# Late position steps of a Fourier mixing layer: spectra requested between the two residual blocks, and VectorE's rows in another order

## The chip, the core and the metric

The kernel runs on one core of a Trainium2 chip. Its engines are TensorE (PE: matmuls, with PEld for its weight loads), VectorE (DVE), ScalarE (ACT), GpSimd (POOL) and SyncE (SP); each works through its own list of instructions in order, and an instruction that has to wait holds up everything behind it on that engine. SP, and here and there ACT and POOL, also issue DMAs. The metric is the device time of one execution in microseconds (us).

## The reference

Two sequences (2048 and 512 positions, 1024 channels, float32) go through two layers and a last norm:

```python
def trunk(x, ...):
    x = x + (banded_gqa_with_sink(q, k, v, ...) * silu(gate)) @ w_out   # layer 0, h = rmsnorm(x)
    f = fftn(h in 4 groups of 256 channels, axes=(position, channel), norm="ortho").real
    x = x + (f * silu(h @ w_gate)) @ w_out                               # layer 1, h = rmsnorm(x)
    return rmsnorm(x, final_norm)
```

The change touches only the end of layer 1: the transform over positions, the gate, the out-projection, the residual sum and the last norm.

## The kernel before

**Arithmetic.** A float32 product is made of three matmuls on rounded halves. An operand's high half is a cast on ACT, its low half the remainder, a subtraction on DVE (`halves_of` L1394 to L1408: ACT L1403, DVE L1404; `split` L1015; `own` L1523 and L1524). `matmul3` (L117) multiplies high by high, high by low and low by high, so the second of every three matmuls on TensorE needs the low half.

**The transform over 2048 positions** is split by 16. Earlier steps leave, for each k1 of 0 to 8, two blocks of 128 x 1024 (real and imaginary part of the spectra: `g1r`, `g1s` and so on, made on DVE by the sums and differences of `pm`, L1261). A position step for k1 turns these into the two row blocks k1 and 16-k1. The order of k1 is 0 and 8, 4, 2, 6, 1, 7, 3, 5; the last four, k1 = 1, 7, 3, 5, are the loop at L1844 and are called the late position steps here. The spectra of k1 = 7, 3 and 5 wait their turn in DRAM (`god`): ACT issues their six writes (L1824) during step 6, and `reads` (L1835 to L1842) brings one pair back per step as four DMAs of 256 KB on SP (L1841, tiles `go`).

One late step does this:
1. `halves_of` gives the operands `gp_<half>_<0 or 1>`: half 0 and 1 are channels 0 to 511 and 512 to 1023, 0 and 1 the real and the imaginary spectrum.
2. `position` (L1412 on): for each half, six matmuls of 260 columns and six of 256 with the table `tbp` into PSUM (`ABp_0`, `ABp_1`); copies, sums and differences on ACT and DVE give two blocks `up` (L1441 to L1448); DVE multiplies each by its gate (L1451, `s2p`).
3. PE transposes both in half blocks (`tw`, L95). From them come the operands of the out-projection: `tT` (own halves), `F` (sums), `S` (split sums).
4. The out-projection of the two blocks is done together in `Outs.products` (L1565 on), in the manner of Strassen and Winograd, as seven products of four times three 512-column matmuls; their PSUM tiles are `Wo`, `Zo` and `Xo`. DVE adds each to the residual blocks `xa` and `xb` (L1572; the trace calls them `x`, the order `x_1`, `x_15` by their row blocks).
5. Last norm: ACT squares and sums (`jkf`, L1056), DVE scales the sum (`invf`, L110), POOL raises it to the power -1/2 (L111), DVE scales the block (L1468), SP writes it out (L1470).

The steps are woven together: while step k's seven products run on PE, step k+1's operands are made and its `ABp` matmuls stand between the products. The last product of a step goes into `xb`'s lower half; this sum, the late sum, and xb's norm fall into the following step.

**What sets the order.** A scheduler puts the program into one list per engine; `after` and `seq` (L159 to L168) add dependencies of order alone, with chains "dve" and "act" through the late steps. SP's DMAs go out in the order of its list: one that waits for a buffer or for a block to be ready holds up those behind it. Buffers come from small pools: four tiles `x` are shared by residual blocks and gate tiles, the spectra and `up` blocks share the pool of `zt`, and PSUM has three accumulators (`psum2`) for `Wo`, `Zo`, `Xo` and the earlier `fo`.

`fo` are the plain out-projections of step 2's two blocks (`finish`, L1484 on), 24 matmuls of 512 columns for each half block; step 6's `ABp` matmuls are placed among them.

Of the kernel before, what the change touches and what calls it, by code (L numbers as in the profile page):

```python
# [42 lines left out]
def encoder(  # L43
# [947 lines left out]
    def fourier_phase(tail):  # L991
        with ExitStack() as es:
# [481 lines left out]
            def normed(x2, r):  # L1474
                norm(x2, r)()

            def residual(r):
                x2 = x_tile(f"x2_{r[0]}")
                SP.dma_start(x2, rows(x1d, r))
                return x2  # L1480

            late = [None]
# [1 line left out]
            def finish(uT, r, between=None):  # L1484
                r0 = r[0]
                x2 = residual(r)
                for half in range(2):
                    if half and between:
                        chain["turns"] = end
                        between()  # L1490
                    ps = psum2.tile([P, 512], F32, tag="acc", name=f"fo{r0}_{half}")
                    for k in range(KD):
                        first_one = k == 0 and half == (between is not None)
                        end = matmul3(
                            ps, uT[k], wo[half * KD + k], k == 0, k == KD - 1, behind=chain.get("turns") if first_one else None
                        )
                    xs = x2[:, half * 512 : half * 512 + 512]
                    DVE.tensor_tensor(xs, xs, ps, ALU.add)
                if between:
                    late[0] = x2, r  # L1500
                else:
                    normed(x2, r)
                return end
# [3 lines left out]
            class Outs:  # L1507
# [57 lines left out]
                def products(self, hooks, last=False):  # L1565
# [48 lines left out]
                        upper()  # L1614
                    if not last:
                        prod(W, A[1, 1], ft["N4"], four, False)
                        seq("dve", add(xb, 0, W))
                        return xb, self.us[1][1]
                    ss = main.tile([P, 8], F32, tag="ss", bufs=2, name="ssl")
                    junk = fp.tile([P, 512], F32, tag="c12", bufs=1, name="jkl").bitcast(BF16)  # L1620

# [193 lines left out]
            o0s, o1s = pm(tsn[1], tsn[3], "o0s")  # L1815
            g1r, g7r = pm(e0c, o0c, "g1r")
            g1s, g7s = pm(o0s, e0s, "g1s")
            g3r, g5r = pm(e1c, o1s, "g3r")
            p6 = [halves_of("p6", *G[6], 0), None]
            g5s, g3s = pm(o1c, e1s, "g5s")  # L1820
            G[1], G[7], G[3], G[5] = (g1r, g1s), (g7r, g7s), (g3r, g3s), (g5r, g5s)
            for k1 in (7, 3, 5):
# [22 lines left out]
            for k1, k2 in ((1, 7), (7, 3), (3, 5), (5, None)):  # L1845
# [3 lines left out]
                def split_g():  # L1849

                    nxt["s"] = [gated(name, r, place) for r, place in zip(tiles, (xtile, left))]
                    scaled = []

                    def weigh():
                        if late[0]:
                            scaled.append(norm(*late[0], "dve"))

                    nxt["p"] = [halves_of(name, *gl, 0, weigh), None]
                    o.rest()
                    for f in scaled:  # L1860
                        f()
                    if not ft["T3"]:
                        f_sums("T3", right)

                def transform(third):
                    if not ft["N4"]:
                        f_sums("N4", left)
                    nxt["p"][1] = halves_of(name, *gl, 1)
                    nxt["o"] = Outs(k1, position(name, k1, *gl, tiles, (nxt["s"], tb), nxt["p"], third))

                def turns():
                    nxt["o"].operands()
                    nxt["o"].load()
                    if k2:
                        nxt["r"] = reads(k2)

                late[0] = o.products((split_g, transform, turns, lambda: nxt["o"].others()))
                o = nxt["o"]
            o.products((lambda: (o.rest(), normed(*late[0])), lambda third: third(), lambda: None), last=True)


    fourier_phase(attention_phase())
# [98 lines left out]
```

## Time and profile before

| | |
|---|---|
| runs | 1584.42, 1585.3 and 1582.39 us, median 1584.42 |
| the profiled execution | 1583.8 us, of which span 1582.0 us |
| TensorE clock granted | 0.999 |
| PE, DVE, ACT, POOL busy | 99%, 73%, 56%, 28% of the span |
| `ABp` matmuls of step 6 | 1428.12 to 1441.6 us |
| of steps 1, 7, 3, 5, the first at | 1460.72, 1485.39, 1511.46, 1536.27 us |

Times in the trace count from the span's start. A line of a timeline reads: start, length, engine, source line, operation, output<-input, shape, how many in the group, and in brackets how long the engine had stood idle ahead of it and on what. Lengths overlap a little where an engine is pipelined, so distances between starts tell more than single lengths.

### The profile page before, as it was taken

How to read it: one execution, taken by the hardware profiler on the slowest of the kernel's cores; microseconds unless marked ns; L12 is line 12 of the kernel's file. 1: busy time of each engine (PE TensorE's matmuls, PEld its weight loads, DVE VectorE, ACT ScalarE, POOL GpSimd, SP SyncE). 2: the span in 40 equal slices, each digit the busy share in tenths (PEclk: the TensorE clock that was granted, in tenths of full speed). 3: DMA queues.
4: the chain of work that ended last, by engine and by line, in shares of the span. 5: the costliest groups of instructions: out<-in, count | busy, mean ns of one | idle time of the engine just before them, and what ended most of it. 6: DMA issues, size and time to landing. Idle time of an engine off the chain costs nothing.

```text
span 1582.0 us, 27728 instructions
## 1 busy us (share of the span) xinstructions
PE 1568.8 (99%) x9882; PEld 1315.8 (83%) x9882; DVE 1151.3 (73%) x2793; ACT 878.1 (56%) x2096; POOL 444.2 (28%) x614
## 2 busy tenths in 40 slices
PE   9999999999999999999999999999999999999998
PEld 7888888888888888988888888888888888887776
DVE  6888556877457886378764577669778878988886
ACT  7788535776246784267751576546555554343343
POOL 2475642421404314024222242223112121111110
PEclk9999999999999999999999999999999999999999
DMA  8597686575856567665659566675557569448752
GB/s 302 205 331 280 227 356 210 210 266 194 303 202 225 207 234 271 214 221 210 251 172 326 205 231 231 236 259 196 191 213 253 180 228 411 171 181 313 278 180 81
DMA packets 100997, 373.91 MB, mean 236 GB/s; under 512 B 11267, under 2 KB 22283, under 8 KB 83452
## 3 DMA queue, kind: packets, MB, share of 16 engines
q1 hardware_dynamic: 83148, 298.17, 52.9%
q0 software_dynamic: 16400, 70.04, 11.4%
q10 hardware_dynamic: 1312, 3.94, 0.7%
q8 instruction: 78, 1.28, 0.3%
q14 instruction: 59, 0.48, 0.1%
HBM read 280.84 MB, written 91.26 MB: 235 GB/s over the span
## 4 chain that ended last, share of the span: by engine, by line
PE 91%; DVE 4%; DMA 2%; ACT 1%; issue 1%; POOL 0%; POOLq 0%; SPq 0%; DVEq 0%; ACTq 0%
PE gp L117 14%; PE qp L117 14%; PE spt L117 11%; PE op L117 7%; PE W L117 7%; PE av L615 6%; PE spt L530 6%; PE fo L117 4%; PE vp L117 3%; PE Z L117 3%; PE pt L589 3%; PE Wo L117 2%; PE z L117 2%; PE X L117 2%; PE ABp L117 1%; PE Zo L117 1%
## 5 line engine op out<-in xcount | busy, mean ns | idle before, releaser
L117 PE MATMUL gp<-h,wg 128*128 128x512 f32 x960 | 237.7, 396 | 0.0
L117 PE MATMUL qp<-h,wq 128*128 128x512 f32 x960 | 237.1, 396 | 0.0
L549 DVE CUSTOM_DVE_ANT_0 S<-spt,b 128x385 f32<-128x385 f32 (+1 forms) x320 | 156.6, 528 | 105.7 <-PE spt L530 68.4
L117 PEld LDWEIGHTS gp<-h,wg 128*128 128x128 f32 x960 | 174.9, 188 | 37.2 <-issue 1.0
L117 PEld LDWEIGHTS qp<-h,wq 128*128 128x128 f32 x960 | 174.9, 188 | 36.6 <-issue 0.2
L557 ACT ACTIVATE S<-S 128x385 f32<-128x385 f32 (+1 forms) x320 | 188.8, 597 | 19.6 <-DVE S L549 19.3
L597 ACT CAST pts<-pt 128x384 fp32r<-128x384 f32 (+1 forms) x240 | 100.5, 457 | 167.6 <-PE pt L589 158.4
L598 DVE TENSOR_TENSOR pts<-pt,pts 128x384 fp32r<-128x384 f32 (+1 forms) x240 | 114.3, 520 | 23.7 <-ACT pts L597 22.7
L117 PE MATMUL spt<-wo,uT 128*128 128x512 f32 x480 | 120.3, 391 | 0.0
L639 POOL TENSOR_TENSOR uT<-o,uT 128x256 fp32r<-128x256 f32 x75 | 55.5, 740 | 229.8 <-ACT uT L638 229.7
L117 PE MATMUL op<-wo,uT 128*128 128x512 f32 x480 | 118.9, 391 | 0.0
L530 PE MATMUL spt<-kwin,qab 64*128 64x384 f32 (+1 forms) x960 | 118.5, 353 | 0.0
L615 PEld LDWEIGHTS av<-pts,v 128*128 128x128 f32 x576 | 101.4, 188 | 18.8
L615 PE MATMUL av<-pts,v 128*128 128x512 f32 (+1 forms) x576 | 115.7, 341 | 0.0
L117 PE MATMUL fo<-wo,tTu 128*128 128x512 f32 x480 | 115.5, 392 | 0.0
L117 PEld LDWEIGHTS op<-wo,uT 128*128 128x128 f32 x480 | 89.4, 188 | 18.5
L117 PEld LDWEIGHTS spt<-wo,uT 128*128 128x128 f32 x480 | 89.1, 188 | 18.3
L117 PEld LDWEIGHTS fo<-wo,tTu 128*128 128x128 f32 x480 | 88.3, 188 | 17.5 <-ACT wo L1722 0.3
L569 DVE TENSOR_SCALAR S<-S 128x384 f32<-128x384 f32 (+1 forms) x192 | 95.8, 499 | 6.8
L530 PEld LDWEIGHTS spt<-kwin,qab 64*128 64x128 f32 x960 | 74.5, 186 | 28.2 <-issue 26.4
L635 POOL TENSOR_TENSOR o<-o,s 128x256 f32<-128x256 f32 x75 | 55.3, 737 | 134.4 <-DVE o L633 134.0
L589 PEld LDWEIGHTS pt<-ident,S 64*128 64x128 f32 x1328 | 78.2, 138 | 4.3 <-issue 2.0
(331 smaller groups left out, 3178.5 us busy)
## 6 DMA issues: line engine op xcount, KB each, us to landing
wo<-wsd SPq DMA_DIRECT2D x32, 1024.0 KB, 4.9
wq<-wsd SPq DMA_DIRECT2D x31, 1024.0 KB, 6.6
wg<-wsd SPq DMA_DIRECT2D x31, 1024.0 KB, 5.3
x<-x1d SPq DMA_DIRECT2D x40, 512.0 KB, 3.5
b<-b21d SPq DMA_DIRECT2D x40, 512.0 KB, 6.6
b<-rowd SPq DMA_DIRECT2D x40, 384.0 KB, 4.3
xs<-in_x_dram SPq DMA_DIRECT2D x23, 512.0 KB, 7.3
s2d<-gt POOLq DMA_DIRECT2D x40, 256.0 KB, 4.7
```

Of the source, the lines that this page charges most:

```text
L117: ins = pe(PE.matmul(out, a[i], b[j], start=start and i + j == 0, stop=stop and i == 1, skip_group_check=more))
L530: pe(PE.matmul(banks[j][:, 2 + k0 * P : 2 + k1 * P], res["q"][rows, qp, b * P : (b + 1) * P], kwin[g][rows, kp, b * P + k0 * P : b * P + k ...
L549: seq(DVE, DVE.tensor_tensor_reduce(out=s[:, e0:e1], in0=ps[:, 1 + e0 : 1 + e1], in1=st["bias"][:, j, 386 - e1 : 386 - e0][:, ::-1], scale ...
L557: last_exp[0] = seq(ACT, ACT.activation(s[:, e0:e1], s[:, e0:e1], AF.Exp, bias=s[:, 386:387], scale=-1.0, accum_out=s[:, 387:388]))
L569: seq(DVE, DVE.tensor_scalar(s[:, ks], s[:, ks], den, None, ALU.mult))
L589: pe(PE.transpose(ps[h][:, kb, j, :], ss[j][rows, 1 + kb * P : 1 + (kb + 1) * P], ident[rows, rows]))
L597: seq(ACT, ACT.copy(hi, ps[:, k0:k1]))
L598: seq(DVE, DVE.tensor_tensor(lo, ps[:, k0:k1], f32(hi), ALU.subtract))
L615: pe(PE.matmul(to, v, pt, start=n == part == 0, stop=part == 1 and n in (1, len(todo) - 1), skip_group_check=n > 1,))
L635: eng.tensor_tensor(o, o, s, ALU.mult)
L639: low = eng.tensor_tensor(lo, o, f32(hi), ALU.subtract)
```

## The change

Four things change, all in order; no arithmetic is added or removed.

1. **Requests.** In a late step SP asked for both residual blocks and then for the next step's spectra. Now it asks for the first block, the spectra, and then the second block.
2. **DVE's order at the head of the steps 7, 3 and 5.** The late sum and its norm stood ahead of this step's first sum; now the first sum and the real spectrum's low half come first, the late sum follows, and the norm of the late block (`invf`) moves behind the imaginary low half and `S`. The low halves of channels 512 to 1023 move ahead of the late block's scaling. In step 1 there is no late sum, since its late block comes from `finish`; `invf` moves there too.
3. **Step 6's operands.** The low halves of channels 0 to 511 were made behind the pair `g3r`, `g5r`; they are now ahead of it, and those of channels 512 to 1023 stand ahead of the pair `g5s`, `g3s`.
4. **The last step**, the seven products of step 5: the first sum into `xa` is now ahead of the late sum.

```diff
-            def residual(r):
+            def residual(r, behind=None):
                 x2 = x_tile(f"x2_{r[0]}")
-                SP.dma_start(x2, rows(x1d, r))
+                after(SP.dma_start(x2, rows(x1d, r)), behind)
...
-                    late[0] = x2, r
+                    late[0] = x2, r, lambda: None
...
                         prod(W, A[1, 1], ft["N4"], four, False)
-                        seq("dve", add(xb, 0, W))
-                        return xb, self.us[1][1]
+                        return xb, self.us[1][1], lambda: seq("dve", add(xb, 0, W))
...
+            p6 = [halves_of("p6", *G[6], 0), None]
             g3r, g5r = pm(e1c, o1s, "g3r")
-            p6 = [halves_of("p6", *G[6], 0), None]
+            p6[1] = halves_of("p6", *G[6], 1)
             g5s, g3s = pm(o1c, e1s, "g5s")
...
-                    scaled = []
-                    def weigh():
-                        if late[0]:
-                            scaled.append(norm(*late[0], "dve"))
-                    nxt["p"] = [halves_of(name, *gl, 0, weigh), None]
-                    o.rest()
-                    for f in scaled:
-                        f()
+                    xb, r, whole = late[0]
+                    nxt["p"] = [halves_of(name, *gl, 0, whole)]
+                    o.halve(3)
+                    scaled = norm(xb, r, "dve")
+                    o.own(1, 1)
+                    nxt["p"].append(halves_of(name, *gl, 1))
+                    scaled()
...
-                    nxt["p"][1] = halves_of(name, *gl, 1)
...
-                    nxt["o"].operands()
-                    nxt["o"].load()
+                    new = nxt["o"]
+                    new.operands()
+                    new.x2 = [residual(new.us[0][1])]
                     if k2:
                         nxt["r"] = reads(k2)
+                    new.x2.append(residual(new.us[1][1], last_read[0]))
...
-            o.products((lambda: (o.rest(), normed(*late[0])), lambda third: third(), lambda: None), last=True)
+            def old():
+                xb, r, whole = late[0]
+                whole()
+                o.rest()
+                normed(xb, r)
+            o.products((old, lambda third: third(), lambda: None), last=True)
```

DVE at the head of step 7 before the change. `x_10` is the late block (the second of step 6), `x_1` and `x_15` are the first and second block of step 1, whose products run here; `gp` are step 7's low halves.

```order
L1524 TENSOR_TENSOR tT_01_16934<-tw_16853,tT_01_16934 128x512
L1572 TENSOR_TENSOR x_10_16687<-x_10_16687,Wo_16691 128x512
L1572 TENSOR_TENSOR x_1_16904<-x_1_16904,Wo_16950 128x512
L1404 TENSOR_TENSOR gp_0_0_16969<-go_0_16908,gp_0_0_16969 128x512
L110 TENSOR_SCALAR invf_16975<-ssf_16972 128x1
L1404 TENSOR_TENSOR gp_0_1_16978<-go_1_16909,gp_0_1_16978 128x512
L1015 TENSOR_TENSOR S_1_16981<-F_1_16894,S_1_16981 128x512
L1524 TENSOR_TENSOR tT_11_16984<-tw_16870,tT_11_16984 128x512
L1468 TENSOR_SCALAR x_10_16687<-x_10_16687,invf_16975,gfb 128x1024
L1572 TENSOR_TENSOR x_15_16906<-x_15_16906,Zo_16951 128x512
L1404 TENSOR_TENSOR gp_1_0_17002<-go_0_16908,gp_1_0_17002 128x512
L1404 TENSOR_TENSOR gp_1_1_17005<-go_1_16909,gp_1_1_17005 128x512
```

The same place after the change:

```order
L1524 TENSOR_TENSOR tT_01_16934<-tw_16853,tT_01_16934 128x512
L1572 TENSOR_TENSOR x_1_16904<-x_1_16904,Wo_16949 128x512
L1404 TENSOR_TENSOR gp_0_0_16968<-go_0_16906,gp_0_0_16968 128x512
L1572 TENSOR_TENSOR x_10_16687<-x_10_16687,Wo_16691 128x512
L1404 TENSOR_TENSOR gp_0_1_16972<-go_1_16907,gp_0_1_16972 128x512
L1015 TENSOR_TENSOR S_1_16975<-F_1_16894,S_1_16975 128x512
L110 TENSOR_SCALAR invf_16981<-ssf_16978 128x1
L1524 TENSOR_TENSOR tT_11_16984<-tw_16870,tT_11_16984 128x512
L1404 TENSOR_TENSOR gp_1_0_16987<-go_0_16906,gp_1_0_16987 128x512
L1404 TENSOR_TENSOR gp_1_1_16990<-go_1_16907,gp_1_1_16990 128x512
L1468 TENSOR_SCALAR x_10_16687<-x_10_16687,invf_16981,gfb 128x1024
L1572 TENSOR_TENSOR x_15_16914<-x_15_16914,Zo_16950 128x512
```

`invf`, which waits for ACT's sum of squares of `x_10`, was ahead of `gp_0_1` and is now two rows behind it; `gp_1_0` and `gp_1_1` are ahead of the scaling of `x_10` and of the sum into `x_15`. Steps 3 and 5 read alike with other blocks.

DVE in step 6 before: the four low halves `gp` among the pairs that make the spectra of k1 = 7, 3 and 5 (`od_0`, `o0s`, `g3r`, `g5s` and `tc` are such spectra on their way to `god`).

```order
L1261 TENSOR_TENSOR g1s<-o0s,e0s 128x1024
L1261 TENSOR_TENSOR g3r<-od_0_16146,od_1_16152 128x1024
L1261 TENSOR_TENSOR o0s<-o0s,e0s 128x1024
L110 TENSOR_SCALAR invf_16401<-ssf_16398 128x1
L1261 TENSOR_TENSOR od_0_16146<-od_0_16146,od_1_16152 128x1024
L1468 TENSOR_SCALAR x_12_16344<-x_12_16344,invf_16401,gfb 128x1024
L1404 TENSOR_TENSOR gp_0_0_16427<-ev_1_15654,gp_0_0_16427 128x512
L1404 TENSOR_TENSOR gp_0_1_16430<-ev_1_15658,gp_0_1_16430 128x512
L1261 TENSOR_TENSOR g5s<-tc_16160,od_1_16148 128x1024
L1404 TENSOR_TENSOR gp_1_0_16469<-ev_1_15654,gp_1_0_16469 128x512
L1261 TENSOR_TENSOR tc_16160<-tc_16160,od_1_16148 128x1024
L1404 TENSOR_TENSOR gp_1_1_16472<-ev_1_15658,gp_1_1_16472 128x512
```

And after:

```order
L1261 TENSOR_TENSOR g1s<-o0s,e0s 128x1024
L1404 TENSOR_TENSOR gp_0_0_16424<-ev_1_15654,gp_0_0_16424 128x512
L1261 TENSOR_TENSOR o0s<-o0s,e0s 128x1024
L110 TENSOR_SCALAR invf_16401<-ssf_16398 128x1
L1404 TENSOR_TENSOR gp_0_1_16427<-ev_1_15658,gp_0_1_16427 128x512
L1468 TENSOR_SCALAR x_12_16344<-x_12_16344,invf_16401,gfb 128x1024
L1261 TENSOR_TENSOR g3r<-od_0_16146,od_1_16152 128x1024
L1404 TENSOR_TENSOR gp_1_0_16433<-ev_1_15654,gp_1_0_16433 128x512
L1261 TENSOR_TENSOR od_0_16146<-od_0_16146,od_1_16152 128x1024
L1404 TENSOR_TENSOR gp_1_1_16436<-ev_1_15658,gp_1_1_16436 128x512
L1261 TENSOR_TENSOR g5s<-tc_16160,od_1_16148 128x1024
L1498 TENSOR_TENSOR x_2_16512<-x_2_16512,fo_0_16514 128x512
```

All four low halves now lie further up; `g3r`, `od_0` and the last difference `tc` (the row behind this piece) lie further down, and so do the DMAs that write them. On PE, `ABp_0`'s first low-half matmul in step 6 stands behind 11 `fo` matmuls instead of 32. Of the two half blocks into which step 6's `ABp` are woven, 18 `fo` matmuls instead of 6 are left behind the last of `ABp_1`.

SP, the requests of step 1 before (`x_1` and `x_15` the residual blocks, `go` step 7's spectra, the last row the output of `x_6`):

```order
L1479 DMA x_1_16904<-x1d 128x1024
L1479 DMA x_15_16906<-x1d 128x1024
L1841 DMA go_0_16908<-god_0_150 128x512
L1841 DMA go_1_16909<-god_1_151 128x512
L1841 DMA go_0_16908<-god_0_150 128x512
L1841 DMA go_1_16909<-god_1_151 128x512
L1470 DMA out_dram<-x_6_16685 128x1024
```

And after:

```order
L1479 DMA x_1_16904<-x1d 128x1024
L1841 DMA go_0_16906<-god_0_150 128x512
L1841 DMA go_1_16907<-god_1_151 128x512
L1841 DMA go_0_16906<-god_0_150 128x512
L1841 DMA go_1_16907<-god_1_151 128x512
L1479 DMA x_15_16914<-x1d 128x1024
L1470 DMA out_dram<-x_6_16685 128x1024
```

`x_15` has moved behind the four reads. The steps after it have the same pattern, `x_7` and `x_9`, then `x_3` and `x_13`.

## The prediction

> **What bounds the kernel now.** I read the page's head first: nothing but TensorE can be the bound over the whole.
>
> ```profile
> span 1582.0 us, 27728 instructions
> PE 1568.8 (99%) x9882; PEld 1315.8 (83%) x9882; DVE 1151.3 (73%) x2793; ACT 878.1 (56%) x2096; POOL 444.2 (28%) x614
> ```
>
> PE is busy for 99% of the span, so an order of rows can win only where PE stands idle. Next come PE's waits from 1420 us on, the part that the change touches (columns: total us, times, longest).
>
> ```profile
> PE ABp L117 <- DVE gp L1404: 3.0, 5, 1.1
> PE ABp L117 <- DVE invf L110: 0.7, 1, 0.7
> ```
>
> Six waits, 3.7 us, all of `ABp` on VectorE: one in step 6, one in step 1 (put down to `invf`), two in step 7, one each in 3 and 5. The list leaves out short gaps, so I price the matmuls and measure what is lost from start to start. The prices, from three groups in PE's timeline that follow each other without a gap:
>
> ```profile
> 1364.42 11.19 PE L117 MATMUL fo<-wo,tTu 128*128 128x512 f32 x48
> 1375.45 3.06 PE L117 MATMUL ABp<-gp,tbp 128*128 128x260 f32 x24
> 1378.34 11.07 PE L117 MATMUL fo<-wo,tTu 128*128 128x512 f32 x48
> ```
>
> A 512-column matmul takes (1375.45 - 1364.42)/48 = 0.230 us, one of `ABp` (1378.34 - 1375.45)/24 = 0.120 us.
>
> **Term 1: step 7.** PE's timeline where its `ABp` begin:
>
> ```profile
> 1484.26 1.30 PE L117 MATMUL Zo<-fT,S 128*128 128x512 f32 x5
> 1485.39 0.28 PE L117 MATMUL ABp<-gp,tbp 128*128 128x260 f32 x1
> 1485.80 0.96 PE L117 MATMUL Wo<-fT,S 128*128 128x512 f32 x3
> ...
> 1488.47 1.23 PE L117 MATMUL ABp<-gp,tbp 128*128 128x260 f32 x8 [1.12 <-DVE gp L1404]
> ...
> 1492.07 1.82 PE L117 MATMUL ABp<-gp,tbp 128*128 128x260 f32 x11 [0.41 <-DVE gp L1404]
> ```
>
> The five `Zo` end at 1484.26 + 5 x 0.230 = 1485.41. Up to the low-half matmul at 1492.07 come 12 of `ABp_0` (1.44), 12 of `Wo` (2.76) and one of `ABp_1` (0.12): without a stall it would start at 1489.73. Lost: 2.34 us. What VectorE and ScalarE did meanwhile, from their timelines:
>
> ```profile
> 1482.99 0.68 DVE L1524 TENSOR_TENSOR tT<-tw,tT 128x512 fp32r<-128x512 f32 x1
> 1484.46 1.28 DVE L1572 TENSOR_TENSOR x<-x,Wo 128x512 f32<-128x512 f32 x2 [0.78 <-PE Wo L117]
> 1485.66 0.69 DVE L1404 TENSOR_TENSOR gp<-go,gp 128x512 fp32r<-128x512 f32 x1
> 1487.66 0.15 DVE L110 TENSOR_SCALAR invf<-ssf 128x1 f32<-128x1 f32 x1 [1.32 <-ACT jkf L1056]
> 1487.74 0.68 DVE L1404 TENSOR_TENSOR gp<-go,gp 128x512 fp32r<-128x512 f32 x1
> 1489.54 1.28 DVE L1468 SCALAR_TENSOR_TENSOR x<-x,invf,gfb 128x1024 f32<-128x1024 f32 x1
> 1490.73 0.68 DVE L1572 TENSOR_TENSOR x<-x,Zo 128x512 f32<-128x512 f32 x1
> 1491.33 1.29 DVE L1404 TENSOR_TENSOR gp<-go,gp 128x512 fp32r<-128x512 f32 x2
> 1483.26 1.27 ACT L1403 CAST gp<-go 128x512 fp32r<-128x512 f32 x2 [1.74 <-DMA go<-god]
> 1486.48 1.06 ACT L1056 ACTIVATE jkf<-x 128x1024 bf16<-128x1024 f32 x1
> ```
>
> A 512-element row takes 0.60 of VectorE from start to start (1485.66 less 1484.46, two rows), a 1024-element one about 1.19 (1490.73 less 1489.54). The idle 0.78 and 1.32 are the fault: the late sum, first in line, waits for the product just finished, and `invf`, ahead of the imaginary low half, waits for ScalarE's squares. In the new order the sum into `x_1` starts at 1483.59, `gp_0_0` at 1484.19 (its cast ends at about 1483.88), the late sum at 1484.79 (its product has long let go of PE: the old start, 1484.46, shows it there), `gp_0_1` at 1485.39, done by 1486.07, `S` at 1485.99, `invf` not after 1487.66, `tT` 0.60, and then `gp_1_0` and `gp_1_1` from about 1488.4 to 1489.7. PE asks for `gp_0_0`'s low half at 1485.53, for `gp_0_1`'s, behind three more of `ABp` and two or three of `Wo`, at about 1486.4, and for `gp_1_0`'s at 1489.73, by then 0.7 us old. Also, `Wo` at 1485.80 stood behind the old first sum (the second of the pair at 1484.46, which reads the accumulator that `Wo` goes on with); that sum is now over by 1484.3. All 2.34 us go. Late next is `gp_0_1`, with some 0.3 us to spare. What is made later instead, the scaling of `x_10` and the sum into `x_15`, has no PE row waiting for it: its output and the buffer follow some 0.5 us later, and the residual block that takes the buffer is added a step later.
>
> **Terms 2 and 3: steps 3 and 5.**
>
> ```profile
> 1510.32 1.30 PE L117 MATMUL Zo<-fT,S 128*128 128x512 f32 x5
> 1516.88 1.83 PE L117 MATMUL ABp<-gp,tbp 128*128 128x260 f32 x11 [0.42 <-DVE gp L1404]
> 1541.70 1.82 PE L117 MATMUL ABp<-gp,tbp 128*128 128x260 f32 x11 [0.40 <-DVE gp L1404]
> ```
>
> By the same 25 matmuls the second row would start at 1510.32 + 1.15 + 4.32 = 1515.79: 1.09 lost, of which the list shows 0.42. Step 5's wait is like it (0.40), so I take 1.09 again. The spectra are in earlier there, so nothing new stands ahead of the low halves, and both go. The lower end counts shown waits alone: 1.12 + 0.41 + 0.42 + 0.40 = 2.35 for the three steps in place of 4.52.
>
> **The requests.** SP's timeline and waits, and the traffic in the stretch of step 1's requests (columns from the second: us, then busy us of PE, PEld, DVE, ACT, POOL, the clock, the DMA share, GB/s):
>
> ```profile
> 1475.36 1.95 SPq L1841 DMA_DIRECT2D go<-god  x4
> SPq L1841 <- PE tw L95: 6.6, 3, 2.3
> 1468.00:1485.00 17.00, 17.00 (x103) 13.91 (x102) 13.50 (x23) 6.88 (x15) 2.16 (x3) 1.00 1.01 384
> ```
>
> The reads wait for the transposes, which free their buffers, not for the block ahead of them, so they leave no earlier. In the queue they lie ahead of 512 KB more: at 384 GB/s, 1.3 us at most, and ScalarE's cast at 1483.26 may start by so much sooner. VectorE reaches `gp_0_0` at 1484.19 in either case: worth 0. The second block lands later by the reads' 1 MB at most, 2.7 us; its first sum is the `Zo` row at 1490.73, more than 5 us behind the reads' end: cost 0. Behind it in SP's list is `x_6`'s output, which waits for its own scaling.
>
> **Step 6.**
>
> ```profile
> 1428.12 0.41 PE L117 MATMUL ABp<-gp,tbp 128*128 128x260 f32 x2
> 1436.48 0.63 PE L117 MATMUL ABp<-gp,tbp 128*128 128x260 f32 x3 [0.66 <-DVE gp L1404]
> 1429.40 1.22 DVE L1261 TENSOR_TENSOR g1s<-o0s,e0s 128x1024 f32<-128x1024 f32 x1
> 1435.73 1.28 DVE L1404 TENSOR_TENSOR gp<-ev,gp 128x512 fp32r<-128x512 f32 x2
> ```
>
> PE now asks after 11 `fo` instead of 32: at 1428.12 + 0.24 + 2.53 = 1430.89. VectorE makes `gp_0_0` right behind `g1s`, until about 1431.2: a stall of 0.3 in place of 0.66. The other three low halves come 0.5 us or more before PE asks, if POOL's power for `x_12` is quick; each can cost some tenths if not. Bounds: a gain of 0.66, or a loss of 10 `fo` matmuls, 2.3 us. I take a gain of 0.3, but it is not in the sum, because step 1 stands behind something else.
>
> **Step 1.** The row put down to `invf`, the sum ahead of it on VectorE, and what that waits for:
>
> ```profile
> 1461.74 1.89 PE L117 MATMUL ABp<-gp,tbp 128*128 128x260 f32 x11 [0.73 <-DVE invf L110]
> 1460.39 0.69 DVE L1572 TENSOR_TENSOR x<-x,Wo 128x512 f32<-128x512 f32 x1 [3.21 <-DMA x<-x1d]
> 1449.69 10.61 DMA x<-x1d
> 1441.00:1460.00 19.00, 19.00 (x114) 15.71 (x113) 14.10 (x25) 9.62 (x19) 2.42 (x3) 1.00 1.02 403
> 1431.79 0.33 ACTq L1824 DMA_DIRECT2D god<-g3r  x1
> 1439.93 0.33 ACTq L1824 DMA_DIRECT2D god<-tc  x1
> god<-tc ACTq DMA_DIRECT2D x1, 512.0 KB, 7.6
> ```
>
> `invf` is not the cause: VectorE stood 3.21 us for the residual block `x_6`, requested at 1449.69 and 10.61 us under way, with the DMA engines full (share 1.02). That block still comes first in step 1. So what counts is when it lands, and a gain of PE ahead of it turns into a longer wait here. The new step 6 makes `g3r` and `od` about 4 us later and the last difference `tc` about 1.2 us later, and their writes go out later, nearer to the full stretch. A write of 512 KB is 1.3 us of it at 403 GB/s. Also, `x_2`'s output, the SP row ahead of `x_6`, reuses the completion semaphore of `tc`'s write and so waits until that has landed. Ends: 1.3 earlier (if a write less lies ahead of it) to 2.6 later (two writes pushed into the full stretch). I take half a write, 0.6 later, since most of the moved writes still find room before 1441, and count it in full.
>
> [...]
>
> **The last step** loses nothing and may gain the wait for `x_13`'s sum; no row shows one, so 0.
>
> **Sum.** -2.34 - 1.09 - 1.09 + 0.6 = -3.9 us against the profiled execution of 1583.8 (span 1582.0 and 1.8 around it): 1579.9. The median of the runs shown, 1584.42, is 0.6 above the profiled one, so for a median I say 1580.5, 0.25% faster. A difference under 0.2%, 3.2 us, is about what a measurement of this kernel cannot tell from none; the border is at 1581.25.
>
> **Rivals.**
> - *Step 1 gives back what 7, 3 and 5 win.* `x_6` lands 1.5 to 2.6 us later than before. For it: the full DMA engines and the 3.21 us wait, so every microsecond counts. Against it: a third of the DMA share was free before 1441. Time: 1584.4 - 4.5 + 1.5 to 2.6, 1581.4 to 1582.5, within 0.2%. Shown waits alone (-2.35 + 0.6) give 1582.7, the same verdict.
> - *The change does not do what it says in step 7,* because the spectra and not VectorE set it: the cast waited 1.74 us for them. If they land no sooner and another 1.3 us late (the queue fuller), `gp_0_0` moves to 1485.2, about 1.3 of term 1 is lost: 1581.8.
> - *Slower: the semaphore line on SP.* `x_2`'s output waits for `tc`'s write; `x_6`, `x_10`, the gate tile, the weights of the later products and the next requests all stand behind it. If the later write takes long, SP stands, and step 1 moves one for one. Above 4.5 us of delay the gain is gone, from 7.7 us on it is slower by over 0.2%, 1587.6 and more. For it: 7.6 us for a write in the full stretch. Against it: before, the write issued at 1439.93 had landed two us ahead of 1449.69; it would have to land at 1457.
>
> **Chances.** Forecast (gain 3.2 to 5) 0.62, giving 1579.4 to 1581.2; step 1 gives back, or shown waits alone, 0.20; step 7 unmoved 0.08; slower 0.10. The range to 1584 leaves out the slower case, and at 1577.5 takes in `x_6` 1.3 earlier with a last bit of step 6 (4.5 + 1.3 + 0.6, and 0.5 for what a median scatters).
>
> **What would show it.** Right: no `ABp` wait on `gp` in the steps 7, 3 and 5, 25 matmuls in 4.3 us from the end of `Zo`; the two sums no longer a pair; `invf` behind `S`; the reads still on `tw`; `x_6`'s DMA row near 11 us and a wait of 0.7 to 2 us ahead of step 1's low-half matmul. Wrong: `x_6` landing after 1463, SP idle on `god<-tc`, a wait for `x_15` ahead of the sum with `Zo`, or new stalls in step 6 beyond 1 us.

## The result and the profile after

The changed kernel takes 1579.78 us (median of 22 runs, 1578.44 to 1582.02) where the kernel before takes 1583.37 (22 runs, 1582.06 to 1585.3). The ratio is 0.9978, 95% interval 0.9972 to 0.9984: 0.22% faster, 3.6 us. The forecast was 1580.5, a range of 1577.5 to 1584.0, and "faster by over 0.2%" at 0.62; that border lies inside the measured interval.

The profiled execution has this head and these waits of TensorE from 1420 us on (total us, times, longest):

```profile
span 1579.2 us, 27736 instructions
PE 1568.1 (99%) x9882; PEld 1317.5 (83%) x9882; DVE 1151.0 (73%) x2793; ACT 878.5 (56%) x2096; POOL 443.5 (28%) x614
PE ABp L117 <- DVE gp L1404: 2.4, 3, 2.0
```

Of the six waits three are left: two short ones in step 6 (0.22 and 0.17) and one in step 1, which has grown from 0.73 to 1.98. Steps 7, 3 and 5 have none. PE's timeline at the head of step 7:

```profile
1487.26 1.30 PE L117 MATMUL Zo<-fT,S 128*128 128x512 f32 x5
1488.39 0.65 PE L117 MATMUL ABp<-gp,tbp 128*128 128x260 f32 x4
1488.88 0.63 PE L117 MATMUL Wo<-fT,S 128*128 128x512 f32 x2
1489.35 1.12 PE L117 MATMUL ABp<-gp,tbp 128*128 128x260 f32 x8
1490.30 2.46 PE L117 MATMUL Wo<-fT,S 128*128 128x512 f32 x10
1492.60 1.61 PE L117 MATMUL ABp<-gp,tbp 128*128 128x260 f32 x12
1494.04 2.91 PE L117 MATMUL Zo<-wo,S 128*128 128x512 f32 x12
```

From the first `ABp` at 1488.39 to `Zo` at 1494.04 pass 5.65 us; 24 matmuls at 0.120 and 12 at 0.230 are 5.64. Not a tenth is lost any more. VectorE at the same place shows the new order, with no idle time noted ahead of any row:

```profile
1486.60 0.68 DVE L1572 TENSOR_TENSOR x<-x,Wo 128x512 f32<-128x512 f32 x1
1487.19 0.68 DVE L1404 TENSOR_TENSOR gp<-go,gp 128x512 fp32r<-128x512 f32 x1
1487.79 0.68 DVE L1572 TENSOR_TENSOR x<-x,Wo 128x512 f32<-128x512 f32 x1
1488.39 0.68 DVE L1404 TENSOR_TENSOR gp<-go,gp 128x512 fp32r<-128x512 f32 x1
1488.99 0.68 DVE L1015 TENSOR_TENSOR S<-F,S 128x512 fp32r<-128x512 f32 x1
1489.74 0.15 DVE L110 TENSOR_SCALAR invf<-ssf 128x1 f32<-128x1 f32 x1
1489.81 0.68 DVE L1524 TENSOR_TENSOR tT<-tw,tT 128x512 fp32r<-128x512 f32 x1
1490.41 1.28 DVE L1404 TENSOR_TENSOR gp<-go,gp 128x512 fp32r<-128x512 f32 x2
1491.61 1.28 DVE L1468 SCALAR_TENSOR_TENSOR x<-x,invf,gfb 128x1024 f32<-128x1024 f32 x1
```

Step 1 looks otherwise. PE, and VectorE's sum into `x_6` ahead of the low halves:

```profile
1461.05 0.28 PE L117 MATMUL ABp<-gp,tbp 128*128 128x260 f32 x1
1463.31 2.68 PE L117 MATMUL ABp<-gp,tbp 128*128 128x260 f32 x11 [1.98 <-DVE gp L1404]
1465.79 3.60 PE L117 MATMUL Wo<-fT,S 128*128 128x512 f32 x12
1469.22 1.61 PE L117 MATMUL ABp<-gp,tbp 128*128 128x260 f32 x12
```

```profile
1461.96 0.69 DVE L1572 TENSOR_TENSOR x<-x,Wo 128x512 f32<-128x512 f32 x1 [4.70 <-DMA x<-x1d]
```

The wait is 1.25 us longer. The matmuls behind it are also slow: 11 of `ABp` take 2.48 us (1.72 before), 12 of `Wo` 3.43 (2.75 before). The windows of this execution say why; columns from the second are us, busy us of PE, PEld, DVE, ACT, POOL, the granted clock, DMA share, GB/s:

```profile
1460.44:1463.85 3.41, 1.43 (x8) 0.91 (x6) 1.89 (x4) 0.00 (x0) 0.00 (x0) 1.00 0.93 290
1463.85:1467.26 3.41, 3.41 (x13) 3.06 (x13) 3.41 (x7) 0.44 (x2) 0.56 (x1) 0.50 1.03 422
```

For 3.41 us TensorE was granted half its clock.

To see where the time went, cut PE's timeline at rows that both kernels have: the first `ABp` of step 6, the first `Wo` of its products, the first `ABp` of step 1, then each `Zo<-wo` (one follows the `ABp` of each step, the fifth stands in the last step). "Step 7" is then the stretch from step 1's `Zo<-wo` to step 7's. In us:

| stretch | before | after | difference |
|---|---|---|---|
| step 6 to its products | 27.17 | 27.17 | 0.00 |
| W and Z up to step 1 | 5.44 | 5.44 | 0.00 |
| step 1 | 6.95 | 9.62 | +2.67 |
| step 7 | 26.06 | 23.38 | -2.68 |
| step 3 | 24.82 | 23.39 | -1.43 |
| step 5 | 24.81 | 23.38 | -1.43 |
| last step, and what follows to the end | 38.62 | 38.44 | -0.18 |

The sum is -3.05; step 6 began 0.31 later in this execution (1428.43 against 1428.12), which the change does not touch. So 5.7 us are won behind step 1, and step 1 gives back up to 2.7.

### The profile page after: what moved, and what is told of

The parts are those of the page before. It is cut to its first block, busy times and chain, and to the rows that moved or that the text cites. A ratio compares the mean times of both kernels' runs of the same rounds, so it can differ in the third digit from the quotient of the medians.

```text
span 1579.2 us, 27736 instructions
## 1 busy us (share of the span) xinstructions
PE 1568.1 (99%) x9882; PEld 1317.5 (83%) x9882; DVE 1151.0 (73%) x2793; ACT 878.5 (56%) x2096; POOL 443.5 (28%) x614
## 3 DMA queue, kind: packets, MB, share of 16 engines
q0 software_dynamic: 16400, 70.04, 11.4%
## 4 chain that ended last, share of the span: by engine, by line
PE 93%; DVE 4%; DMA 2%; issue 1%; ACT 1%; POOL 0%; SPq 0%; POOLq 0%; DVEq 0%; ACTq 0%
PE gp L117 14%; PE qp L117 14%; PE spt L117 11%; PE op L117 7%; PE W L117 6%; PE av L615 6%; PE spt L530 6%; PE vp L117 3%; PE Z L117 3%; PE Wo L117 3%; PE pt L589 3%; PE fo L117 3%; PE z L117 2%; PE X L117 2%; PE Zo L117 2%; PE ABp L117 1%
```

## The experiments

Each kernel below gets the same table row from its own profile: step 1, then the steps 7, 3 and 5, and the ratio to the kernel before, timed on the same chip (its median was 1582.97 to 1583.37 from one chip to the next, so medians of different rows compare to some 0.4 us). In all of them step 6 takes between 27.12 and 27.17 us. The theory at the start: step 6's new order makes `x_6` land late and costs step 1 all 2.7 us, by way of a semaphore. The rivals: the new row order in step 1 itself costs it; the slow clock has a cause of its own.

| kernel | step 1 | 7 / 3 / 5 | median | ratio (95%) |
|---|---|---|---|---|
| before | 6.95 | 26.06 / 24.82 / 24.81 | 1583.37 | 1 |
| changed | 9.62, clock halved | 23.38 / 23.39 / 23.38 | 1579.78 | 0.9978 (0.9972 to 0.9984) |
| step 6 put back | 6.88 | 23.38 / 23.39 / 23.39 | 1578.21 | 0.9973 (0.9963 to 0.9983) |
| step 6 alone | 9.50, clock halved | 24.82 / 24.82 / 24.82 | 1585.50 | 1.0017 (1.0008 to 1.0026) |
| requests put back | 7.83 | 23.38 / 23.37 / 23.38 | 1579.17 | 0.9974 (0.9963 to 0.9984) |
| filler for PE | 6.06 (and 1.79 of filler) | 23.38 / 23.37 / 23.39 | 1579.83 | 0.9979 (0.9969 to 0.9989) |
| step 1's low halves first | 5.71 | 23.53 / 23.50 / 23.39 | 1577.37 | 0.9962 (0.9949 to 0.9976) |
| both: that, and step 6 put back | 5.64 | 23.39 / 23.39 / 23.38 | 1577.40 | 0.9962 (0.9949 to 0.9976) |
| `tc` on POOL's queue | 7.92 | 23.38 / 23.38 / 23.39 | 1578.93, one run | none |
| late sum put back | 8.03 | 23.77 / 23.77 / 23.77 | 1580.33 | 0.9983 (0.9974 to 0.9992) |
| `tc` behind `x_6` | 6.78 | 23.38 / 23.39 / 23.38 | 1577.68 | 0.9967 (0.9955 to 0.9979) |
| upper low halves put back | 8.04 | 24.17 / 24.23 / 24.22 | 1582.04 | 0.9996 (0.9987 to 1.0005) |
| one write more | 8.97 | 23.38 / 23.39 / 23.38 | 1581.62 | 0.9989 (0.9980 to 0.9998) |

### Step 6 put back, and step 6 alone

```diff
-            p6 = [halves_of("p6", *G[6], 0), None]
             g3r, g5r = pm(e1c, o1s, "g3r")
-            p6[1] = halves_of("p6", *G[6], 1)
+            p6 = [halves_of("p6", *G[6], 0), None]
```

> The changed kernel with step 6's four low halves put back where they were; requests and late steps stay changed. In the trace of the changed kernel step 1 starts its low halves 1.25 us later than before relative to the work ahead of it, and its next 23 matmuls run at a granted clock of 0.61 and 0.78, together 2.7 us. Theory: both come from step 6 (tc's write later, x_2's output held by it, x_6 requested later, a wait of 2.0 us instead of 0.7). Then x_6's request goes out near 1449.7 again, the wait ahead of step 1's low halves is about 0.7 us, the clock stays 1.00, and the time is 2.7 us under the changed kernel's 1579.8, about 1577.1. Rival: step 1's own new order on VectorE (invf behind S) or the late steps cost it; then the wait stays near 2 us and the time at 1579.8.

The second kernel is the one before with the opposite edit.

> The kernel before with step 6's part of the change alone. Theory: x_6 lands 1.2 us later, step 1 loses 2.7 us, the stalls in steps 7, 3 and 5 stay: 1583.4 + 2.7 = 1586.1. Rival: step 6's shorter stalls (0.66 to 0.39 us) reach the end and nothing is lost in step 1: 1583.1.

PE in step 1, first with step 6 put back, then with step 6 alone, and for the latter the window behind the wait:

```profile
1461.22 1.82 PE L117 MATMUL ABp<-gp,tbp 128*128 128x260 f32 x11 [0.74 <-DVE gp L1404]
```

```profile
1462.82 1.89 PE L117 MATMUL ABp<-gp,tbp 128*128 128x260 f32 x11 [1.70 <-DVE invf L110]
1464.55 4.51 PE L117 MATMUL Wo<-fT,S 128*128 128x512 f32 x12
```

```profile
1464.62:1468.03 3.41, 3.41 (x10) 2.64 (x10) 3.01 (x5) 0.54 (x2) 0.00 (x0) 0.50 0.79 316
```

Step 1's loss follows step 6's order in both directions: 6.88 without it, 9.50 with it in a kernel whose late steps are unchanged. The rival that step 1's own order costs it has fallen. Step 6 alone makes the kernel before slower, 2.5 us by the medians (1582.97 to 1585.50; 2.7 expected). Putting it back gains less in the timed runs than the 2.7 us expected: 1578.21 in place of 1577.1. The two profiles of kernels with the new step 6 seen so far had the halved clock; the timed runs show that many have not (they are counted in the last section).

Step 6 alone shows one more thing. Its late steps have the old order, and yet step 7 takes 24.82, like the steps 3 and 5, and not 26.06. ScalarE's casts of step 7's spectra and VectorE's `invf` in this kernel:

```profile
1484.30 1.24 ACT L1403 CAST gp<-go 128x512 fp32r<-128x512 f32 x2
1489.10 0.15 DVE L110 TENSOR_SCALAR invf<-ssf 128x1 f32<-128x1 f32 x1
```

In the kernel before, the cast waited 1.74 us for the reads and `invf` 1.32 for ScalarE's squares, which stand behind the casts. Here the reads landed 6.4 us after their request in place of 8.0 (medians of four), and neither row waits. So, by these two profiles, 1.24 us of step 7's stall in the kernel before came from spectra that landed late. In this profile the loss of 2.55 in step 1 and the 1.24 leave 1.3 us.

### The requests put back

```diff
-                    new.x2 = [residual(new.us[0][1])]
+                    new.load()
                     if k2:
                         nxt["r"] = reads(k2)
-                    new.x2.append(residual(new.us[1][1], last_read[0]))
```

> The changed kernel with SP's old order of requests, both residual blocks ahead of the spectra. Theory: the reads wait for the transposes in both orders, so nothing changes: 1579.8 within 0.6. Rival: the spectra need the earlier place; step 7's real low half comes late and a stall of up to 1.3 us on gp comes back: 1581.1.

The three steps take 23.37 to 23.39 us in either order of requests, and the ratio is that of the changed kernel within its interval. The order of the requests is worth nothing. This execution also shows step 1 without the slow clock: a wait of 1.69 us, and 7.83 in place of 9.62.

### A filler for TensorE

```diff
                     hooks[0]()
-                    prod(Z, S[1], ft["T1"], four, True)
+                    end = prod(Z, S[1], ft["T1"], four, True)
+                    if self.n == 6:
+                        ones = nc.const_aps.tensor(1.0, [P, 512], BF16)
+                        ps = filler[0].tile([P, 512], F32, tag="fill", name="fill")
+                        for _ in range(9):
+                            end = after(PE.matmul(ps, ones[:, :P], ones, start=True, stop=True), end)
...
```

> The changed kernel with nine matmuls of constants, 512 columns, into a spare PSUM bank between step 1's Zo and its first ABp, some 2.1 us of work for TensorE in the time in which it stood waiting; the outputs are the same. Theory: the clock of 0.61 follows from the 2.0 us wait; with the filler the low half still starts near 1463.3, but at clock 1.00, and the 1.4 us that the slow matmuls cost are gone: 1578.4. Rival: the clock falls in this place for another reason; the slow matmuls stay and the time is 1579.8 or a few tenths more.

PE's timeline with the filler:

```profile
1462.41 2.14 PE L1585 MATMUL fill<-const-bfloat16-1.0 128*128 128x512 bf16 x9
1464.20 2.04 PE L118 MATMUL ABp<-gp,tbp 128*128 128x260 f32 x12
1466.08 2.90 PE L118 MATMUL Wo<-fT,S 128*128 128x512 f32 x12
```

The matmuls behind the filler run at full clock, as the theory has it (12 of `Wo` are 2.90 us long here, 3.60 in the changed kernel). But filler and step 1 together take 1.79 + 6.06 = 7.85, which is no less than the 7.83 of a kernel that had waited at full clock, and the median did not fall (1579.83). In its profile step 6 began 1.4 us later than in the changed kernel, for a reason that lies ahead of everything changed here; it stays open. So its median tells nothing of what the clock costs. But none of its nine timed executions has a mean clock under 0.999, against eight of 22 of the changed kernel at 0.998, which is in favour of the theory.

### What makes x_6 late: a semaphore or the bytes

The chain of the changed kernel names a semaphore. `tc`'s write landed at 1450.30 and `x_2`'s output, which had been waiting for it, went out at 1450.37, with `x_6`'s request behind it. Two rows of the chain of waits, and from the list of waits that of SP's queue:

```profile
1441.44 8.87 DMA god<-tc
1450.80 11.07 DMA x<-x1d
```

```profile
SPq L1470 <- DMA god<-tc: 1.6, 1, 1.6
```

The next kernel lets POOL issue that write.

```diff
-                    ACT.dma_start(t, g)
+                    (POOL if t is god[3][1] else ACT).dma_start(t, g)
```

> The changed kernel with the last spectrum's write (tc) issued by POOL on its own queue, which shares no completion semaphore with SP's DMAs. Theory: x_2's output then goes out as soon as x_2 is scaled, some 0.7 us sooner, x_6 with it, and the wait ahead of step 1's low halves falls from 2.0 to about 1.3 us, at clock 1.00. Rival: the semaphore is not the cause; x_6's request stays near 1450.8 us and the wait near 2 us.

Its chain and PE's timeline:

```profile
1449.08 11.96 DMA x<-x1d
```

```profile
1462.47 1.82 PE L117 MATMUL ABp<-gp,tbp 128*128 128x260 f32 x11 [1.79 <-DVE gp L1404]
```

The request did go out sooner: 21.25 us after step 6's first `ABp` (1427.83) in place of 22.37. But the load then took 11.96 in place of 11.07, and the wait is 1.79. The semaphore theory has fallen: it holds the request, not the landing. What holds the landing shows in the traffic, over the first 12.88 us of step 6 and from there to `x_6`'s landing. First the kernel before, then the changed one:

```profile
1428.12:1441.00 12.88, 12.22 (x62) 9.93 (x61) 12.44 (x15) 2.32 (x5) 1.40 (x1) 1.00 0.66 244
1441.00:1460.30 19.30, 19.30 (x116) 15.93 (x115) 14.10 (x25) 9.62 (x19) 2.42 (x3) 1.00 1.02 401
```

```profile
1428.43:1441.31 12.88, 12.49 (x65) 9.96 (x64) 12.44 (x15) 2.60 (x6) 0.86 (x1) 1.00 0.58 196
1441.31:1461.87 20.56, 20.02 (x115) 16.20 (x113) 14.05 (x25) 9.26 (x18) 3.32 (x3) 1.00 1.03 408
```

In the first stretch the changed kernel moves 196 x 12.88 = 2.52 MB, the one before 3.14. The missing 0.62 MB are 1.5 us at 408 GB/s, and in the second stretch the DMA engines are full in both (share 1.02 and 1.03). The full stretch is 1.26 us longer. Up to the landing of `x_6` both kernels have moved the same, 10.9 MB (3.14 + 7.74 and 2.52 + 8.39), and so has the one with POOL's write (329 GB/s over 33.21 us). To test that, `tc`'s write goes behind the requests of `x_6` and `x_10`, on SP:

```diff
                 for t, g in zip(god[k1], G[k1]):
-                    ACT.dma_start(t, g)
+                    if t is not god[3][1]:
+                        ACT.dma_start(t, g)
...
             o.load()
+            after(SP.dma_start(god[3][1], G[3][1]), asked[10])
```

> The changed kernel with the last spectrum's write (tc, 512 KB) issued by SP right behind the requests of x_6 and x_10, so that these bytes no longer lie ahead of x_6. The run with tc on POOL's queue sent x_6's request out 1.1 us sooner and x_6 landed only 0.2 us sooner, so the semaphore theory has fallen. Theory now: the DMA engines are full from about 1441 us on, and x_6 lands when all bytes issued ahead of it have moved; in the first 12.9 us of step 6 the changed kernel moves 2.5 MB where the one before moved 3.1. Then 512 KB less ahead of x_6 is 1.3 us at 408 GB/s: the wait ahead of step 1's low halves falls from 2.0 to about 0.7 us, the clock stays 1.00, step 1 takes about 6.9 us in place of 9.6 (7.8 where the clock held): 1578.2. Rival: x_6's own way takes 11 us whatever lies ahead; the wait stays near 1.7 us or more.

Chain and PE's timeline again:

```profile
1449.04 10.86 DMA x<-x1d
```

```profile
1461.33 1.83 PE L117 MATMUL ABp<-gp,tbp 128*128 128x260 f32 x11 [0.65 <-DVE gp L1404]
```

With 512 KB less ahead of it `x_6` lands 1.3 us sooner than in the changed kernel (32.09 us after step 6's first `ABp`, in place of 33.44), the wait is 0.65, and step 1 takes 6.78. The request went out no sooner than in the kernel with POOL's write (21.23 and 21.25): the bytes made the difference; up to the landing 10.6 MB were moved (330 GB/s over 32.09 us). And with 512 KB more, `tc` written a second time to a spare place right behind the first write:

```diff
...
                     ACT.dma_start(t, g)
+                    if t is god[3][1]:
+                        ACT.dma_start(spare, g)
```

> The changed kernel with the last spectrum written a second time, to a spare place in DRAM, right behind the first write: 512 KB more ahead of x_6. [...] The time rises by 1.3 us for the wait and by up to another 1 us because the changed kernel pays the slow clock in only a part of its runs: 1581 to 1582. Rival: the wait does not grow with the bytes, or the slow clock in the two profiles had nothing to do with the wait: step 1 below 9 us, 1580 or less.

PE's timeline, and the two windows that hold the wait:

```profile
1465.04 1.84 PE L118 MATMUL ABp<-gp,tbp 128*128 128x260 f32 x11 [2.82 <-DVE gp L1405]
```

```profile
1460.39:1463.80 3.41, 1.83 (x9) 1.28 (x7) 0.11 (x1) 0.44 (x1) 0.00 (x0) 1.00 1.03 392
1463.80:1467.22 3.42, 2.19 (x14) 1.91 (x15) 3.42 (x7) 0.26 (x1) 0.56 (x1) 1.00 0.92 326
```

The wait grew to 2.82 us, 0.84 more (512 KB at 408 GB/s are 1.3), and the time to 1581.62, as expected. `x_6` landed 0.8 us later than in the changed kernel (34.25 us after step 6's first `ABp`), behind 11.4 MB (333 GB/s). Its request, held by the second write, also went out 1.5 us later (23.85 in place of 22.37), so this run does not separate bytes and request as the two before it do. In the profiled execution the clock did not fall: this longest wait of all was paid at full clock (1.00 in both windows), and step 1 took 8.97. In the timed runs it did more often than not: eight of the eleven executions have a mean clock of 0.998 or less. Wait and clock are taken up again at the end.

### Which row of VectorE's new order wins what

The late sum (`ahead` here) put back ahead of the first sum:

```diff
-                    nxt["p"] = [halves_of(name, *gl, 0, whole)]
+                    nxt["p"] = [halves_of(name, *gl, 0)]
...
+                    if ahead:
+                        ahead()
                     seq("dve", add(xa, 0, W))
...
```

> The changed kernel with the late sum put back ahead of the first sum in steps 7, 3 and 5; the norm stays behind S, and the low halves of channels 512 to 1023 ahead of the scaling. Theory: the late sum waits for its product, so the first sum and gp_0_0 slip, PE waits about 0.8 us for gp_0_0's low half in each of the three steps, and no more: 2.4 us slower than the changed kernel, 1582.2; the three steps take 24.2 us in place of 23.4 each. Rival: only the place of invf counts, steps of 23.4 to 23.6 us: 1580.

The low halves of channels 512 to 1023 put back behind the scaling and the sum with `Zo`:

```diff
-                    nxt["p"].append(halves_of(name, *gl, 1))
                     scaled()
...
+                    nxt["p"].append(halves_of(name, *gl, 1))
                     nxt["o"] = Outs(k1, position(name, k1, *gl, tiles, (nxt["s"], tb), nxt["p"], third))
```

> The changed kernel with the low halves of channels 512 to 1023 put back behind the late block's scaling and the sum with Zo. With the late sum put back, the steps 7, 3 and 5 took 23.77 us instead of 23.38, so that row is worth 0.4 us each; the remaining 1.04 us of steps 3 and 5 and 2.3 of step 7 belong to the place of invf and of these low halves. Theory: invf does it; the low halves come 1.8 us later on VectorE, 0.1 to 0.3 us after PE asks for them: steps of 23.6 us, 0.7 us slower than the changed kernel in all. Rival: the low halves' place does it: steps of 24.4 us in 3 and 5, 3 us slower in all.

VectorE with the late sum put back, and then PE in step 3 with the upper low halves put back:

```profile
1485.43 1.28 DVE L1572 TENSOR_TENSOR x<-x,Wo 128x512 f32<-128x512 f32 x2 [0.78 <-PE Wo L117]
```

```profile
1514.62 0.28 PE L117 MATMUL ABp<-gp,tbp 128*128 128x260 f32 x1
1515.25 1.83 PE L117 MATMUL ABp<-gp,tbp 128*128 128x260 f32 x11 [0.35 <-DVE gp L1404]
1516.91 2.91 PE L117 MATMUL Zo<-wo,S 128*128 128x512 f32 x12
```

The late sum is worth 0.39 us a step, half of what I expected: the 0.78 of idle time returns, but the scheduler then also puts three of `Wo` ahead of the first low half, and they cover a part. The upper low halves are worth 0.79 in step 7 and 0.84 in the other two. I had expected 0.2; the rival was nearer. (Of this kernel's 8.04 in step 1, 0.3 is the edit's own: the second 12 `ABp` take 1.74 there in place of 1.45.) From 1514.62 to 1516.91 the 12 matmuls take 2.29 us in place of 1.44: the first low half comes 0.51 late (0.63 less 0.12), and the 11 matmuls behind it take 1.66 in place of 1.32, which fits that `gp_1_1` follows one row of 0.60 us later. The profile names 0.35 of these 0.85. If the parts add up, which no run shows, 0.2 us of steps 3 and 5 and 1.5 of step 7 are left for the place of `invf`, whose squares came 1.32 late in step 7. No run moves `invf` alone. The profile of step 6 alone says that 1.24 of the 1.5 are lost only when the spectra land late; with the new place no low half has to wait for the squares.

### Better than both

In step 1 VectorE stands idle for 4.70 us ahead of the sum into `x_6`, with the low halves behind it. Putting them (`ahead` is now the call of `halves_of` for the lower half) ahead, in step 1 alone:

```diff
                     prod(W, A[0, 0], wo[0:4], four, True)
+                    if ahead:
+                        ahead()
                     seq("dve", add(xa, 0, W))
...
```

> The changed kernel, and in step 1 alone the low halves of channels 0 to 511 are also put ahead of the sum into x_6. VectorE is idle for 4.7 us there before x_6 lands, so they are done early, and only the second group of Wo (which goes on with the accumulator that this sum reads) still waits for x_6. Theory: the wait ahead of step 1's low halves goes, 12 ABp (1.44 us) cover it, the clock stays 1.00, and step 1 (first ABp to the Zo with wo) takes about 6.0 us in place of 9.6 (6.9 in the kernel before): 1576.5. Rival: Wo waits for x_6 as long as the low halves did; step 1 stays above 7.5 us: 1578 or more.

VectorE's timeline in step 1, then PE's:

```profile
1457.09 0.68 DVE L1404 TENSOR_TENSOR gp<-g1r,gp 128x512 fp32r<-128x512 f32 x1
...
1461.23 0.69 DVE L1572 TENSOR_TENSOR x<-x,Wo 128x512 f32<-128x512 f32 x1 [2.86 <-DMA x<-x1d]
```

```profile
1460.54 1.60 PE L117 MATMUL ABp<-gp,tbp 128*128 128x260 f32 x12
1461.98 2.99 PE L117 MATMUL Wo<-fT,S 128*128 128x512 f32 x12
```

Step 1 takes 5.71 us, 0.07 above the price of its matmuls, though `x_6` lands as late as before. And with step 6 put back as well:

> The same with step 6's low halves put back as well, so x_6 is requested 1.1 us sooner. Theory: once nothing but Wo waits for x_6, the earlier landing is worth 0.2 us at most, and step 6 takes 27.2 us in either order: 1576.4, no difference to the kernel without it. Rival: the landing still counts in full: 1 us faster than that kernel.

5.64 and the same median: once only `Wo` waits for `x_6`, it may land a microsecond later. These two kernels, 1577.37 and 1577.40, are 0.38% faster than the kernel before. The 1576.5 expected was 0.9 too low.

## Why the prediction came out

**Terms 1 to 3, steps 7, 3 and 5: right, and each too small by 0.34.** Forecast -2.34, -1.09 and -1.09; measured -2.68, -1.43 and -1.43. The mechanism was as told: no wait, `invf` behind `S`, the two sums apart. What I left out is behind the row at which I stopped counting. I measured up to `ABp_1`'s first low-half matmul. The 11 matmuls from there on took 1.66 us before (1492.07 to 1493.73) and now keep to 1.32, which is the 0.34 of each step. The lower end of 2.35, from shown waits alone, would have missed more than half. One thing the account of term 1 left open: why ScalarE's squares were late in step 7 alone. It names the place of `invf` as the fault, but 1.24 of the 2.34 came from spectra that landed late, by the profile of step 6 alone; the rival on step 7 had that cause right, and the stall went all the same because no low half stands behind `invf` any more.

**The requests: right.** Worth 0 by the run with the old order. The reads still waited for the transposes, and the second block kept nothing waiting.

**Step 6: right for the time, wrong by its own term.** I took 0.3 us of gain ahead of step 1. There is none; step 6 takes 27.17 in either order, although the waits that the profile names there fell from 0.66 to 0.39. (In the trace 16 `fo`, not 18, follow the last of `ABp_1` in the two half blocks.)

**Step 1: the mechanism half right, the size wrong.** The failed term is "+0.6, half a write". Writes were pushed into the full stretch, as said, but more than a whole write: 0.62 MB, 1.26 us in the profiled execution (0.95 with the requests put back). "Most of the moved writes still find room" was the wrong step: I counted the free share before 1441 as if it could still be used, but a write can't start before its spectrum is made, and the free time lay ahead of that. The semaphore on `x_2`'s output, which I gave as a second cause and as the slower rival, does hold the request and is not what counts: with `tc` on POOL the request went out 1.12 us sooner and the load landed 0.2 sooner. And the wait of 1.98 us was followed by 3.41 us at a clock of 0.50, which no term had.

**Why the total was near all the same.** In the steps and at the end 5.7 us were won in place of 4.5; step 1 cost 0.9 to 1.1 where the clock held (7.83 to 8.03 against 6.95) and 2.7 where it fell, in place of 0.6. From the medians' -3.6, the timed runs lost about 2.1 in step 1, an estimate; 0.4 of it is the profiled execution of the kernel before, which lay that far above its median. The rest, 1.7, is what a mixture gives: with eight of 22 executions at a mean clock of 0.998, eight times 2.7 and 14 times 1.0 are 1.6 on average. Two errors of over a microsecond were of opposite sign, so that the total came within 0.7 us is in part luck. The first rival, that step 1 gives back what the others win, is what happened in part: `x_6` landed 1.26 us later, less than the 1.5 to 2.6 it was given, but where the clock fell, step 1 gave back 2.7; only the win it was set against was larger. The carrying over to the median was off too: I took the runs shown, 1584.42, 0.6 above the profiled execution; over 22 runs the median is 1583.37, 0.4 below.

## What to carry to other kernels

Price the work at a stall from start to start, by unit prices, up to the next row that can't be late, and not to the end of the first wait: a named wait of 0.4 us stood for 1.4. When work that produces data for a DMA is moved later, count the bytes that no longer fit ahead of a full stretch: a load behind them landed later here by about their time at the full rate (0.8 to 1.3 us for 512 KB), while asking for it 1.1 us sooner won 0.2. And a load that is late did little harm here (0.07 us) once only its own sum and the work that needs this sum stood behind it.

## What the hardware showed that I had not expected

Two waits of TensorE were followed by 3.41 us at a clock of 0.50: those of 1.98 us (changed) and 1.70 us (step 6 alone). The waits of 1.60, 1.69, 1.79, 1.88 and 2.82 us in other profiles were not. Length alone does not decide. The halved stretch is 3.41 us long in both, and in the traces of the changed kernel and the one before the stretches between changes of the granted clock are whole multiples of it: 3.413, 109.226 and 1457.491 us in the changed kernel, 1573.544 in the one before, which are 1, 32, 427 and 461 times 3.4133. So the table takes windows of that length, counted from the clock's rise at the start, and gives the busy time of PE in the window that holds the wait. The profile's busy time also counts matmuls that were stretched by waiting for operands (11 `ABp` in 1.73 us behind the wait of step 6 alone, where their price is 1.32), so the fourth column has the same work at the prices of 0.120 and 0.230, an estimate:

| kernel | wait | PE busy in that window | at the prices, about | next window's clock |
|---|---|---|---|---|
| changed | 1.98 | 1.43 of 3.41 | 1.1 | 0.50 |
| step 6 alone | 1.70 | 1.76 | 1.4 | 0.50 |
| requests put back | 1.69 | 1.75 | 1.6 | 1.00 |
| late sum put back | 1.88 | 1.81 | 1.65 | 1.00 |
| one write more | 2.82, over two windows | 1.83 and 2.19 | 1.7 and 1.8 | 1.00 and 1.00 |
| `tc` on POOL's queue | 1.79, over two windows | 2.47 and 2.57 | 2.3 and 2.2 | 1.00 and 1.00 |

One more window is at hand, at the end of the kernel with the upper low halves put back, where PE runs out of work:

```profile
1571.19:1574.60 3.41, 1.58 (x14) 1.38 (x12) 2.11 (x8) 1.65 (x7) 0.49 (x1) 1.00 0.38 154
1574.61:1578.02 3.41, 0.00 (x0) 0.00 (x0) 1.01 (x3) 0.51 (x1) 0.05 (x1) 1.00 0.45 156
```

Busy for 1.58 (1.4 at the prices), and the next window has the full clock. So PE's busy time as the profile has it does not decide: 1.76 was followed by the half clock, 1.75 and 1.58 were not. At the prices, an estimate, they do not part either: about 1.4 was followed by the half clock with step 6 alone and by the full clock here. Where a window begins against the wait differs from run to run (the wait begins 0.89 us into one in the changed kernel, 1.81 with the late sum put back), and a wait that falls on two windows leaves work in both, which fits the profiled execution of the extra write. All this rests on single profiles, and what decides is not shown.

How often the clock fell can be read from the timed runs, since the mean clock of each execution is on record. One halved window lowers it by 0.5 x 3.41 / 1579 = 0.001: the two profiled executions with one have 0.998, the eleven others 0.999 or 1.000. At 0.998 or less are eight of 22 executions of the changed kernel (median 1581.0, the other fourteen 1579.4), seven of eleven of step 6 alone, eight of eleven with one write more, two of nine with step 6 put back, one of eight with the requests put back, two of eleven with the late sum put back, one of ten with the upper low halves put back, and four of 72 of the kernel before, timed beside the experiments. None are there among the nine of the filler and the 16 of the three kernels with step 1's low halves first, both, and `tc` behind `x_6`. The fall goes with long waits, at a price of about 1.6 us in the changed kernel, but where in a timed execution it happened is not on record, and why the requests put back have one of eight and the changed kernel eight of 22, at waits of 1.69 and 1.98 us in their profiles, stays open.
